# Layer norms that end in their own tile's round, in a four-layer recurrent trunk on one core

## The chip, the core and the metric

The kernel runs on one core of a Trainium2 chip. A core has five engines that run side by side, each with a queue of its own that it works off in order: TensorE (PE in the profile; its weight loads are listed apart as PEld), VectorE (DVE), ScalarE (ACT), GpSimd (POOL) and SyncE (SP), which here only starts transfers. Matrix products are written to PSUM, in eight banks of 128 x 512 numbers; everything else lies in SBUF, 128 partitions wide. Engines wait for one another at semaphores, and a waiting instruction holds up all that is queued behind it on its engine. The metric is device time in microseconds (us) of one execution.

## The reference

One inference step of a trunk over 1024 prompt tokens and 64 sample tokens (8 sequences of 8), with 1024 channels. Two mixers, each followed by a gated convolutional FFN, and after each of the four a layer norm over the channels. Cut to what matters here:

```python
for i in range(DEPTH):                                   # DEPTH = 2
    mix = rglru_mixer(x, ...) if i % 2 == 0 else hgrn2_mixer(x, ...)
    x = layer_norm(ALPHA * x + mix, ln_g[i, 0], ln_b[i, 0])
    f = conv_ffn(x, ...)                                 # 1024 -> 2 x 2816 -> 1024
    x = layer_norm(ALPHA * x + f, ln_g[i, 1], ln_b[i, 1])

def layer_norm(x, g, b):
    mu = mean(x); var = mean((x - mu) ** 2)
    return (x - mu) * rsqrt(var + 1e-5) * g + b
```

The mixers end in a product with a 1024 x 1024 matrix, the FFN in one with 2816 x 1024. All of it is float32 in and out; the kernel splits every operand of a product into a high and a low part and adds three products.

## The kernel before

**Phases.** Phase 0 is the first mixer (up to about 288 us) and its closing norm (to about 350), phase 1 the first FFN (to about 1125), phase 2 the second mixer (to about 1820), phase 3 the second FFN (to the end). Tokens lie in nine tiles: 0 to 7 with 128 prompt tokens each, and tile 8 with the 64 sample tokens. The running sum of a tile is z[:, m], 1024 numbers on each partition, which holds one token.

**A layer norm** is the tail of each of the four parts, and all four go through `ln_pipeline`. A round per tile: `step_m` issues the products of the tile on PE (24 matmuls of 512 columns) and `resid` on DVE, which adds a PSUM bank to z and sums up the row (L433). `nrm_a` (L443 to L446) takes the mean on DVE, squares the row with an accumulated sum on ACT (L444), and forms the reciprocal root by logarithm and exponential (L445, L446). `nrm_b` has four instructions on one number per token (L451 to L454) and (z + mean) * g over the row, in place (L456). `nrm_c` scales the row, adds b, in place (L473), and starts the transfer of the tile to DRAM (L478, or L476 for the output). The order of the tiles is 8, 0, 4, 1, 5, 2, 6, 3, 7 at the two mixers (`sums=True`) and 8, 0, 1, ... 7 at the FFNs.

Before the change the three parts belong to three rounds: in round i stand `nrm_b` of the tile before and `nrm_c` of the one before that, and the turn of the one before that again:

```python
            if 0 <= i - 2 < NT:
                nrm_c(order[i - 2], final)
```

**The turn.** The next part needs channels on partitions. At the first FFN's tail `to_x` transposes a tile on PE (8 transposes, L355), copies the high part on ACT (L357) and the low part on DVE (L358). At a mixer's tail `to_sums` (L363) transposes two tiles mp and mp + 4 (16 transposes, L375), because the FFN's input products are done in a form with seven products of 2 x 2 blocks: it forms seven sums of four blocks b11, b21, b12, b22, in scratch rows t1 to t4 inside z, and writes a high part (ACT, L402) and a low part of each into xa. Four of these sums and three low parts are on DVE, which reads PSUM (L406, L413 to L421), four low parts on POOL (L406).

**PE's order.** PE works in program order, so a turn stands between the products of one tile and those of the next, and waits there for the `nrm_c` of its tile. Turns that are left over are put in `pend` and run in the next part's first product step: the list is emptied by `fill` (one) and `flush` (all). In the FFN's `products` the weights come as seven parts i, and the tokens as two halves c of each token group (columns 0 to 287 and 288 to 543); in the first step c is the outer loop, so (0,0), (1,0), ... (6,0) need the sample tile and the sums of tiles 0, 4, 1, 5 only.

**Weights** come by DMA into `raw` buffers and are converted into a place (`wb`, `wr`, `wxf`, `wxb`): the high part by ACT (L216, L185), the low part by POOL or DVE, by `run["lo"]` (L217, L186). For the FFN's input products each of the seven parts is half a place, and four of them need a sum on POOL first (L176 to L182). `convert` does the next block or part if a place and the raw data are there. Only places of kind "b" are open to a block of the next phase. `pump` is one such try; `release` gives the places of the products done back.

Of the kernel before, what the change touches and what calls it, by code (L numbers as in the profile page):

```python
# [14 lines left out]
ALU = mybir.AluOpType  # L15
# [45 lines left out]
def hawk_hgrn2_convffn_deepnorm_kernel(  # L61
# [301 lines left out]
    def to_sums(mp):  # L363
# [20 lines left out]
        if len(ms) == 2:  # L384


            c0s = ((0, 512, 4096, 4608), (0, 512, 4096, 4608), (8192, 8704, 4096, TW), (2048, 2560, 6144, 6656))[mp]
            s = [zf[:, c0:c0 + 512].rearrange("p (k t) -> p k t", t=n) for c0 in c0s]
        else:
            s = [z[:, ms[0], i * 4 * n:(i + 1) * 4 * n].rearrange("p (k t) -> p k t", t=n) for i in range(4)]  # L390
# [20 lines left out]
        hi(6, b22)  # L411
        lo(0, b11, dve)
# [8 lines left out]
        dve.tensor_tensor(t4, b21, t2, ALU.subtract)  # L421
        hi(5, t4)
        lo(3, t1, pool)
# [24 lines left out]
    def nrm_b(m):  # L448
        r = rows_of(m)
        st = stat[:r, m]  # L450
        dve.tensor_scalar(st[:, 5:6], st[:, 3:4], 1.0 / D, LN_EPS, ALU.mult, ALU.add)  # L451
        dve.scalar_tensor_tensor(st[:, 6:7], st[:, 4:5], st[:, 4:5], st[:, 5:6], ALU.mult, ALU.mult)
        dve.tensor_scalar(st[:, 6:7], st[:, 6:7], -0.5, 1.5, ALU.mult, ALU.add)
        dve.tensor_tensor(st[:, 7:8], st[:, 4:5], st[:, 6:7], ALU.mult)  # L454
        if run.get("end") != m:
            dve.scalar_tensor_tensor(z[:r, m], z[:r, m], st[:, 2:3], gb[:r, 0], ALU.add, ALU.mult)  # L456
            return

        for _, c in END:
            dve.tensor_scalar(z[:r, m, c], z[:r, m, c], st[:, 2:3], st[:, 7:8], ALU.add, ALU.mult)  # L460
        for eng, c in END:
            eng.tensor_tensor(z[:r, m, c], z[:r, m, c], gb[:r, 0, c], ALU.mult)
# [3 lines left out]
    def nrm_c(m, final):  # L466
        r = rows_of(m)
        st = stat[:r, m]
        for eng, c in END if run.get("end") == m else ((dve, slice(0, D)),):
            if run.get("end") == m:  # L470
                eng.tensor_tensor(z[:r, m, c], z[:r, m, c], gb[:r, 1, c], ALU.add)
            else:
                eng.scalar_tensor_tensor(z[:r, m], z[:r, m], st[:, 7:8], gb[:r, 1], ALU.mult, ALU.add)  # L473
# [10 lines left out]
    def ln_pipeline(step_m, junk, final=None, between={}, sums=False):  # L484
# [4 lines left out]
        run["end"] = order[-1] if final == "out" else None  # L489

# [6 lines left out]
        for i in range(NT + 2):  # L497
            def mid():
                if 0 <= i - 1 < NT:
                    nrm_b(order[i - 1])  # L500

            if i < NT:
                if not step_m(order[i], mid):
                    mid()
                pump()
                nrm_a(order[i], junk())
            elif final != "out":

                if i == NT:
                    release(run["held"])  # L510
                lo = run["lo"]
                run["lo"] = pool if sums else dve
                convert()
                mid()
                convert()
                run["lo"] = lo
            if 0 <= i - 2 < NT:
                nrm_c(order[i - 2], final)
            if i >= NT and final == "out":
                mid()  # L520
            run["bank"] = "in"
            if i in between:
                between[i]()
            if final != "out" and 3 <= i < NT:
                turn(order[i - 3])
            run["bank"] = "s"
        if final != "out":
            for m in order[NT - 3:]:
                if not sums or m >= 4:
                    pend.append(lambda m=m: turn(m))  # L530
# [97 lines left out]
    def mix_out(phase, w, z_src, li, es, early=None):  # L628
# [4 lines left out]
        def prod_part(ps, m, ks, ws):  # L633
            if m < NT - 1:
                xt = xm[:, m // 4, :, :, HD + (m % 4) * P:HD + (m % 4 + 1) * P]
                for k in ks:
                    wt = ws[k // 2 - ks[0] // 2]
                    wh = wt[:, 0, (k % 2) * 512:(k % 2 + 1) * 512]
                    wl = wt[:, 1, (k % 2) * 512:(k % 2 + 1) * 512]
                    pe.matmul(ps, lhsT=xt[:, k, 0], rhs=wh, start=(k == 0), stop=False)  # L640
                    pe.matmul(ps, lhsT=xt[:, k, 0], rhs=wl, start=False, stop=False)  # L641
                    pe.matmul(ps, lhsT=xt[:, k, 1], rhs=wh, start=False, stop=(k == KT - 1))  # L642
            else:
                for k in ks:
                    wt = ws[k // 2 - ks[0] // 2]
                    lt = ys[:, k].rearrange("p a b -> p (a b)")
                    for i in range(2):
                        wv = wt[:, i, (k % 2) * 512:(k % 2 + 1) * 512]
                        pe.matmul(ps, lhsT=lt, rhs=wv, start=(k == 0 and i == 0), stop=(k == KT - 1 and i == 1))  # L649
# [64 lines left out]
        def pass1(ws):  # L714
            def step_m(m, mid):
# [5 lines left out]
                if m in (NT - 1, 0):  # L721
                    prod_part(banks[m], m, range(4, KT), ws[2:])
                    resid(m, 1, banks[m], True, acc=True)
                else:
# [286 lines left out]
    def ffn(phase, li, final):  # L1011
# [194 lines left out]
        for p in range(NP):  # L1206
            f0, f1 = 2 * p, 2 * p + 1

            def gates(b, p=p, f0=f0, f1=f1):
# [3 lines left out]
                else:  # L1213
                    fills = {(1, 0): [fill], (5, 0): [flush]}
# [32 lines left out]
        for gi, grp in enumerate(GROUPS):  # L1247
# [27 lines left out]
            else:  # L1275
                def fn(ws, grp=grp):
                    flush()

                    def sm(m, mid):
                        prod(m, 0, grp, [ws[0], ws[2]], False, True)  # L1280
                        mid()
                        prod(m, 1, grp, [ws[1], ws[3]], False, True)
                        return True
# [565 lines left out]
```

## Time and profile before

| what | us |
|---|---|
| median of 3 runs | 2591.05 (2588.37 to 2592.32) |
| the profiled execution | 2598.02 |
| its span, first to last instruction | 2596.2 |
| mean granted TensorE clock in it | 0.982 of full |

In the profile a row of the timeline is: start, duration, engine, line, operation, output <- input, shape, count, and in brackets the idle time of the engine before it with the one that ended it. Neighbouring matmuls overlap in these rows, so a matmul's cost is the distance of two starts. The page names DVE and ACT groups by the line of the helper. Busy times over the whole span: PE 2506.6, DVE 1538.2, POOL 1362.1, ACT 951.2 us.

### The profile page before, as it was taken

The numbers are of one execution on the slowest core, as the hardware profiler recorded it, in microseconds if no ns is written. First come the engines' busy times: TensorE is split into PE (matmuls) and PEld (weight loads), VectorE is DVE, ScalarE is ACT, GpSimd is POOL, SyncE is SP. The second block draws the span as 40 slices with busy tenths as digits, with TensorE's granted clock in tenths as the row PEclk, the third lists the DMA queues.
The fourth block names the chain that finished last, engine by engine and source line by source line (L and its number), as shares of the span: only waits on it lengthen the run. The fifth ranks groups of instructions, "written<-read, shape, count | busy, mean of one in ns | idle before, by whom it ended". The sixth has DMA issues, their size and how long they took to land. (4 is left out here: it accounts for less than half of the span.)

```text
span 2596.2 us, 39881 instructions
## 1 busy us (share of the span) xinstructions
PE 2506.6 (97%) x16007; PEld 2320.0 (89%) x16007; DVE 1538.2 (59%) x2384; ACT 951.2 (37%) x1643; POOL 1362.1 (52%) x1162
## 2 busy tenths in 40 slices
PE   9999979999999999999999999999799999999998
PEld 9999869999999788789999999877699999988886
DVE  5987375565656422568858585976666565662326
ACT  4776243333333111244545353444332333340113
POOL 2534158888876432115444443612788887872321
PEclk9999989999999999999999999999899999999999
DMA  4114122222224422121211111132222222264111
GB/s 132 41 45 161 37 81 63 85 71 84 67 84 166 155 100 83 48 83 45 60 30 49 51 42 51 42 105 83 64 78 83 84 67 84 67 235 153 55 46 73
DMA packets 205839, 209.79 MB, mean 81 GB/s; under 512 B 13201, under 2 KB 167953, under 8 KB 205614
## 3 DMA queue, kind: packets, MB, share of 16 engines
q1 hardware_dynamic: 205654, 207.25, 24.8%
q8 instruction: 126, 2.06, 0.3%
q14 instruction: 59, 0.48, 0.1%
HBM read 159.61 MB, written 47.61 MB: 80 GB/s over the span
## 5 line engine op out<-in xcount | busy, mean ns | idle before, releaser
L217 POOL TENSOR_TENSOR wb<-raw,wb 128x1024 fp32r<-128x1024 f32 (+1 forms) x76 | 199.1, 2622 | 523.1 <-ACT wb L216 293.4
L1084 DVE TENSOR_TENSOR z<-z,ps_f 128x256 f32<-128x256 f32 (+2 forms) x550 | 196.0, 378 | 358.5 <-PE ps_f L1079 301.8
L1079 PE MATMUL ps_f<-xa,wb 128*128 128x288 f32 (+1 forms) x3072 | 402.6, 291 | 4.9 <-POOL xa L406 3.1
L1079 PEld LDWEIGHTS ps_f<-xa,wb 128*128 128x128 f32 x3072 | 394.5, 190 | 8.0 <-POOL xa L406 4.0
L1079 PE MATMUL ps_f<-x,wb 128*128 128x288 f32 (+1 forms) x2496 | 327.4, 291 | 20.7 <-DVE z L1084 18.3
L1079 PEld LDWEIGHTS ps_f<-x,wb 128*128 128x128 f32 x2496 | 322.0, 191 | 21.9 <-DVE z L1084 18.9
L300 PE MATMUL ps_in<-xa,wb 128*128 128x384 f32 (+3 forms) x912 | 307.3, 337 | 8.1 <-ACT y8h L1371 5.9
L302 PE MATMUL ps_in<-xa,wb 128*128 128x384 f32 (+3 forms) x912 | 300.4, 329 | 0.5 <-DVE stat L451 0.5
L301 PE MATMUL ps_in<-xa,wb 128*128 128x384 f32 (+3 forms) x912 | 300.7, 330 | 0.1
L433 DVE SCALAR_TENSOR_TENSOR z<-z,ps_fo 128x512 f32<-128x512 f32 x128 | 87.5, 686 | 288.0 <-PE ps_fo L1184 278.2
L186 POOL TENSOR_TENSOR wb<-raw,wb 128x512 fp32r<-128x512 f32 x116 | 162.4, 1407 | 66.5 <-ACT wb L185 56.2
L186 POOL TENSOR_TENSOR wb<-rawf,wb 128x512 fp32r<-128x512 f32 x116 | 165.6, 1435 | 56.9 <-ACT wb L185 56.9
L300 PEld LDWEIGHTS ps_in<-xa,wb 128*128 128x128 f32 x912 | 173.6, 190 | 12.2 <-ACT y8h L1371 7.3
L1132 DVE SCALAR_TENSOR_TENSOR z<-z,ptf 128x1104 f32<-128x1104 f32 x88 | 182.2, 2070 | 1.6
L301 PEld LDWEIGHTS ps_in<-xa,wb 128*128 128x128 f32 x912 | 173.6, 190 | 1.4 <-DVE xa L358 0.9
L302 PEld LDWEIGHTS ps_in<-xa,wb 128*128 128x128 f32 x912 | 173.3, 190 | 1.6 <-DVE wb L217 1.0
L216 ACT CAST wb<-raw 128x1024 fp32r<-128x1024 f32 (+1 forms) x81 | 79.8, 986 | 233.2 <-issue 119.6
L1079 PE MATMUL ps_f<-xa,wxf 128*128 128x256 f32 (+1 forms) x1152 | 149.8, 288 | 2.6 <-ACT z L1099 2.6
L1079 PEld LDWEIGHTS ps_f<-xa,wxf 128*128 128x128 f32 x1152 | 146.6, 189 | 3.0 <-ACT z L1099 3.0
L185 ACT CAST wb<-rawf 128x512 fp32r<-128x512 f32 x116 | 71.0, 623 | 211.9 <-POOL rawf L182 76.0
L185 ACT CAST wb<-raw 128x512 fp32r<-128x512 f32 x116 | 70.1, 623 | 177.5 <-POOL raw L182 63.7
L1182 PE MATMUL ps_fo<-wb,xa 128*128 128x512 f32 x320 | 126.8, 396 | 3.0 <-DVE z L433 3.0
(508 smaller groups left out, 5664.2 us busy)
## 6 DMA issues: line engine op xcount, KB each, us to landing
raw<-in_ffn_w_in_dram SPq DMA_DIRECT2D x44, 512.0 KB
rawf<-in_ffn_w_in_dram SPq DMA_DIRECT2D x44, 512.0 KB
ysave<-z SPq DMA_DIRECT2D x44, 512.0 KB
raw<-in_hg_w_in_dram SPq DMA_DIRECT2D x32, 512.0 KB
xa<-ysave SPq DMA_DIRECT2D x28, 544.0 KB
zsave<-z SPq DMA_DIRECT2D x24, 512.0 KB
raw<-in_ffn_w_out_dram SPq DMA_DIRECT2D x24, 512.0 KB
z<-zsave SPq DMA_DIRECT2D x24, 512.0 KB
```

What stands on the lines that cost most here:

```text
L185: act.copy(w[:, 0], src)
L186: run["lo"].tensor_tensor(w[:, 1], src, w[:, 0], ALU.subtract)
L216: act.copy(w[:, 0, :n], raw[:, :n])
L217: run["lo"].tensor_tensor(w[:, 1, :n], raw[:, :n], w[:, 0, :n], ALU.subtract)
L300: pe.matmul(ps[:, :n], lhsT=wh, rhs=xh, start=(k == 0), stop=False)
L301: pe.matmul(ps[:, :n], lhsT=wh, rhs=xl, start=False, stop=False)
L302: pe.matmul(ps[:, :n], lhsT=wl, rhs=xh, start=False, stop=(k == KT - 1))
L433: dve.scalar_tensor_tensor(zz, zz, a, ps, ALU.mult, ALU.add, accum_out=stat[:, m, n:n + 1] if acc else None)
L1079: pe.matmul(ps[:, :n], lhsT=l, rhs=r, start=(kk == 0 and i < 4 and l is wh and r is xh), stop=(kk == 3 and l is wl), skip_group_check=(i > ...
L1084: dve.tensor_tensor(d, s, pv(ps), ALU.add)
L1132: dve.scalar_tensor_tensor(c[:, :L], gs[:, i:i + L], w[:, i:i + 1], c[:, :L], ALU.mult, ALU.add)
L1182: pe.matmul(ps, lhsT=yh, rhs=wh, start=a, stop=False)
```

## The change

`ln_pipeline` has no third stage any more. A round issues products, `nrm_a`, `nrm_b`, then the turn of the tile before, then `nrm_c` of its own tile. The four small instructions move from `nrm_b` to `nrm_c`. One turn is left over in `pend` where there were three. In `to_sums` the sum t4 moves from DVE to POOL, for which ACT copies b21 out of PSUM; scratch rows of the first pair move. In the last tile's round at a mixer, the products begin with the weights in places of kind "b", each is given back when its products are issued, and a conversion is tried after two of the four; at an FFN two places are given back between the halves of the last tile.

```diff
-            c0s = ((0, 512, 4096, 4608), (0, 512, 4096, 4608), (8192, 8704, 4096, TW), (2048, 2560, 6144, 6656))[mp]
+            c0s = ((8192, 8704, 0, 512), (0, 512, 4096, 4608), (8192, 8704, 4096, TW), (2048, 2560, 6144, 6656))[mp]
...
         hi(6, b22)
+        act.copy(t4, b21)
...
-        dve.tensor_tensor(t4, b21, t2, ALU.subtract)
+        lo(3, t1, pool)
+        pool.tensor_tensor(t4, t4, t2, ALU.subtract)
         hi(5, t4)
-        lo(3, t1, pool)
...
     def nrm_b(m):
         r = rows_of(m)
+        if run.get("end") != m:
+            dve.scalar_tensor_tensor(z[:r, m], z[:r, m], stat[:r, m, 2:3], gb[:r, 0], ALU.add, ALU.mult)
...
+    def nrm_c(m, final):
+        r = rows_of(m)
         st = stat[:r, m]
         dve.tensor_scalar(st[:, 5:6], st[:, 3:4], 1.0 / D, LN_EPS, ALU.mult, ALU.add)
...
-        for i in range(NT + 2):
...
+        for i, m in enumerate(order):
+            step_m(m)
+            pump()
+            nrm_a(m, junk())
+            nrm_b(m)
+            if i == NT - 1:
+
+                release(run["held"])
                 lo = run["lo"]
                 run["lo"] = pool if sums else dve
-                convert()
-                mid()
-                convert()
+                for _ in range(2):
+                    convert()
                 run["lo"] = lo
...
             if i in between:
                 between[i]()
-            if final != "out" and 3 <= i < NT:
-                turn(order[i - 3])
+            if final != "out" and i:
+                turn(order[i - 1])
             run["bank"] = "s"
+            nrm_c(m, final)
         if final != "out":
-            for m in order[NT - 3:]:
-                if not sums or m >= 4:
-                    pend.append(lambda m=m: turn(m))
+            pend.append(lambda: turn(order[-1]))
...
+                elif m == run["last"]:
+
+                    held = list(run["held"])
+                    js = sorted(range(4), key=lambda j: blocks[held[j]].kind != "b")
+                    ps = sbank("ps_o")
+                    for n, j in enumerate(js):
+                        prod_part(ps, m, (2 * j, 2 * j + 1), [ws[j]], (js[0] * 2, js[3] * 2 + 1))
+                        if blocks[held[j]].kind == "b":
+                            release([held[j]])
+                        if n == 1:
+                            convert()
+                    resid(m, 1, ps, True, acc=True)
...
-                    fills = {(1, 0): [fill], (5, 0): [flush]}
+                    fills = {(3, 0): [flush]}
...
                         prod(m, 0, grp, [ws[0], ws[2]], False, True)
-                        mid()
+                        if m == run["last"]:
+                            release([run["held"][0], run["held"][2]])
+                            convert()
                         prod(m, 1, grp, [ws[1], ws[3]], False, True)
```

More of the change, by code (lines that the diff above doesn't have):

```diff
@@ L449, in nrm_b @@
         r = rows_of(m)
+        if run.get("end") != m:
+            dve.scalar_tensor_tensor(z[:r, m], z[:r, m], stat[:r, m, 2:3], gb[:r, 0], ALU.add, ALU.mult)
+    END = (pool, slice(768, D)), (dve, slice(0, 768))
+    def nrm_c(m, final):
+        r = rows_of(m)
         st = stat[:r, m]
@@ L454, in nrm_b @@
         dve.tensor_tensor(st[:, 7:8], st[:, 4:5], st[:, 6:7], ALU.mult)
[L455 to L462, printed above, removed]
-    END = (pool, slice(768, D)), (dve, slice(0, 768))
-    def nrm_c(m, final):
-        r = rows_of(m)
-        st = stat[:r, m]
+        if run.get("end") == m:
+            for _, c in END:
+                dve.tensor_scalar(z[:r, m, c], z[:r, m, c], st[:, 2:3], st[:, 7:8], ALU.add, ALU.mult)
+            for eng, c in END:
+                eng.tensor_tensor(z[:r, m, c], z[:r, m, c], gb[:r, 0, c], ALU.mult)
         for eng, c in END if run.get("end") == m else ((dve, slice(0, D)),):
@@ L489, in ln_pipeline @@
         run["end"] = order[-1] if final == "out" else None
+        run["last"] = order[-1]
         def turn(m):
@@ L495, in turn @@
                 to_sums(m - 4)
-        for i in range(NT + 2):
[L498 to L503, printed above, removed]
-                    mid()
[L505 to L510, printed above, removed]
+        for i, m in enumerate(order):
[5 more added lines that the diff above has]
+                release(run["held"])
                 lo = run["lo"]
                 run["lo"] = pool if sums else dve
-                convert()
-                mid()
-                convert()
+                for _ in range(2):
+                    convert()
                 run["lo"] = lo
[L517 to L520, printed above, removed]
             run["bank"] = "in"
@@ L631, in mix_out, with prod_part @@
         banks = {}
-        def prod_part(ps, m, ks, ws):
+        def prod_part(ps, m, ks, ws, ends=(0, KT - 1)):
             if m < NT - 1:
@@ L639, in prod_part @@
                     wl = wt[:, 1, (k % 2) * 512:(k % 2 + 1) * 512]
-                    pe.matmul(ps, lhsT=xt[:, k, 0], rhs=wh, start=(k == 0), stop=False)
+                    pe.matmul(ps, lhsT=xt[:, k, 0], rhs=wh, start=(k == ends[0]), stop=False)
                     pe.matmul(ps, lhsT=xt[:, k, 0], rhs=wl, start=False, stop=False)
-                    pe.matmul(ps, lhsT=xt[:, k, 1], rhs=wh, start=False, stop=(k == KT - 1))
+                    pe.matmul(ps, lhsT=xt[:, k, 1], rhs=wh, start=False, stop=(k == ends[1]))
             else:
@@ L648, in prod_part @@
                         wv = wt[:, i, (k % 2) * 512:(k % 2 + 1) * 512]
-                        pe.matmul(ps, lhsT=lt, rhs=wv, start=(k == 0 and i == 0), stop=(k == KT - 1 and i == 1))
+                        pe.matmul(ps, lhsT=lt, rhs=wv, start=(k == ends[0] and i == 0), stop=(k == ends[1] and i == 1))
         def prod(m, n, ws):
@@ L714, in pass1, with step_m @@
         def pass1(ws):
-            def step_m(m, mid):
+            def step_m(m):
                 if m == NT - 1:
@@ L1277, in fn, with sm @@
                     flush()
-                    def sm(m, mid):
+                    def sm(m):
                         prod(m, 0, grp, [ws[0], ws[2]], False, True)
-                        mid()
+                        if m == run["last"]:
+                            release([run["held"][0], run["held"][2]])
+                            convert()
                         prod(m, 1, grp, [ws[1], ws[3]], False, True)
-                        return True
                     ln_pipeline(sm, lambda: fs_["junk"], final, {1 + 2 * g: (lambda g=g: states(g)) for g in range(3)})
```

## The prediction, made before the changed kernel was run

> **What bounds the kernel now.** I read the busy shares first, then PE's waits by the line waited for (total, times, longest), then PE's timeline where those waits lie.
>
> ```profile
> PE 2506.6 (97%) x16007; PEld 2320.0 (89%) x16007; DVE 1538.2 (59%) x2384; ACT 951.2 (37%) x1643; POOL 1362.1 (52%) x1162
> ...
> PE ps_f L1079 <- DVE z L1084: 18.3, 2, 10.1
> PE ps_t L375 <- DVE z L473: 14.2, 4, 5.0
> ```
>
> PE is busy almost throughout, so what counts is what adds to its 90 us of idle time or takes from it. The two largest waits are at one place that occurs twice: where a mixer's closing norm passes into the FFN. PE there, first occurrence: the last tile's products start at 339.71, the first seven FFN products run from 345.38 to 384.04; the last row is a stretch of 4 us:
>
> ```profile
> 338.86 1.09 PE L375 MATMUL ps_t<-ident,z 128*128 128x128 f32 x8 [2.13 <-DVE z L473]
> ...
> 339.71 0.48 PE L640 MATMUL ps_o<-wr,xa 128*128 128x512 f32 x1
> ...
> 345.38 1.94 PE L1079 MATMUL ps_f<-xa,wb 128*128 128x288 f32 x13
> ...
> 376.51 3.25 PE L1079 MATMUL ps_f<-x,wb 128*128 128x288 f32 x12 [8.18 <-DVE z L1084]
> ...
> 384.04 1.69 PE L1079 MATMUL ps_f<-xa,wb 128*128 128x256 f32 x13
> 386.56 4.45 PE L1079 MATMUL ps_f<-xa,wb 128*128 128x256 f32 x35 [0.82 <-POOL xa L406]
> ...
> 356.00:360.00 4.00, 3.95 (x17) 3.60 (x17) 3.55 (x5) 0.82 (x3) 3.07 (x2) 0.50 0.32 131
> ```
>
> From the last norm product to the end of (6,0), 345.38 to 384.04, pass 38.7 us. At full clock the work is 7 x 1.69 + two turns of 1.7 = 15.2 us; the rest, 23.5, is idle time (8.18 in the row of 376.51, and L375's longest wait of 5.0) and, after that, a clock of 0.50 (the stretch row's column behind POOL). The waits come twice each, so some 47 us are on offer at the two places. The question is whether DVE, which ends those waits, is relieved. Its rows in a round there, with ACT and POOL between:
>
> ```profile
> 325.69 1.28 DVE L473 SCALAR_TENSOR_TENSOR z<-z,stat,gb 128x1024 f32<-128x1024 f32 x1
> ...
> 334.97 1.31 POOL L406 TENSOR_TENSOR x<-z,x 128x512 fp32r<-128x512 f32 x1
> ...
> 335.25 1.04 DVE L454 TENSOR_TENSOR stat<-stat 128x1 f32<-128x1 f32 x1
> 336.21 1.27 DVE L456 SCALAR_TENSOR_TENSOR z<-z,stat,gb 128x1024 f32<-128x1024 f32 x1
> 337.41 0.20 DVE L443 TENSOR_SCALAR stat<-stat 128x1 f32<-128x1 f32 x1
> ...
> 337.65 1.15 ACT L444 ACTIVATE junk<-z,stat 128x1024 f32<-128x1024 f32 x1 [4.23 <-DVE stat L443]
> 338.70 0.19 ACT L444 ACTIVATION_READ_ACCUMULATOR junk<-z,stat 128x1 f32 x1
> 338.73 0.68 DVE L433 SCALAR_TENSOR_TENSOR z<-z,ps_o 128x512 f32<-128x512 f32 x1
> 339.25 0.20 ACT L446 ACTIVATE stat<-stat 128x1 f32<-128x1 f32 x1
> ...
> 340.02 0.16 DVE L454 TENSOR_TENSOR stat<-stat 128x1 f32<-128x1 f32 x1
> ...
> 341.42 1.28 DVE L473 SCALAR_TENSOR_TENSOR z<-z,stat,gb 128x1024 f32<-128x1024 f32 x1
> ```
>
> DVE is already the bound of these rounds: from one L473 to the one two rounds on, 325.69 to 341.42, pass 15.7 us, where PE needs 2 x 5.6 + 1.7 = 12.9. And it goes from L443 over an L473 of 1.2 to the next L433 (338.73) while ACT still squares, because `nrm_b` and `nrm_c` belong to earlier tiles.
>
> **The change part by part.**
>
> *The added wait.* L456 writes z in place, and L444 reads z. With both in one round, L456 cannot start before the square is over: 337.41 to 338.89 in the rows, 1.5 us after L443 starts. DVE has nothing else to do in that time, as its queue is in order; behind L456 stand the turn's low parts, the small ones, L473, and the next tile's resid, and PE's transposes wait for L473. The trace has no L456 that waits so. Bounds: nothing, if the wait ended with L443; 2.0 us, if it reached to L446's end. I take 1.5, the end of the reads.
>
> One tile's chain is then resid 0.7 + 1.5 + L456 1.2 + four small 0.65 + L473 1.2 = 5.3 us (distances of starts), plus the turn's part of DVE before the small ones.
>
> *First FFN's tail (turn of every tile).* The rows of before:
>
> ```profile
> 1071.68 0.20 DVE L443 TENSOR_SCALAR stat<-stat 64x1 f32<-64x1 f32 x1
> 1071.98 2.40 POOL L217 TENSOR_TENSOR wb<-raw,wb 128x1024 fp32r<-128x1024 f32 x1 [2.80 <-ACT wb L216]
> ...
> 1104.57 0.82 ACT L1198 COPY so<-ps_fs 18x512 f32<-18x512 f32 x2
> ...
> 1108.04 1.03 PE L355 MATMUL ps_t<-ident,z 128*128 128x128 f32 x8
> 1112.90 1.29 DVE L358 TENSOR_TENSOR xa<-ps_t,xa 128x512 fp32r<-128x512 f32 x2 [1.16 <-ACT xa L357]
> ...
> 1121.61 0.47 PE L300 MATMUL ps_in<-xa,wb 128*128 128x512 f32 x1
> ...
> 1128.33 1.23 DVE L217 TENSOR_TENSOR wb<-raw,wb 128x1024 fp32r<-128x1024 f32 x1
> ...
> 1139.58 0.36 PE L300 MATMUL ps_in<-xa,wb 128*128 128x256 f32 x1
> ```
>
> PE needs 6.4 us a round (1108.04 to 1121.61 is two rounds and a turn of 0.8) and does not wait. With the change DVE's round is two resids 1.4 + 1.5 + 1.2 + L358 1.2 + 0.65 + 1.2 = 7.2 to 7.3, and 8.05 in the rounds where L1198's copies stand ahead of the turn's high parts on ACT. PE may now be only one round ahead of a tile's L473, so DVE's pace becomes PE's. From the rows: tile 8 has L443 at 1071.7; its L456 comes behind POOL's L217 (until 1074.4), its L473 ends at 1077.4. Then tile 0 (state copies, short turn) 7.6, tile 1 7.3, tile 2 8.05, tile 3 7.3, tile 4 8.05, tiles 5 and 6 7.3 each: tile 6 ends at 1130.3, its transposes at 1131.1, and only then the next part's first product, which began at 1121.61. 1.6 us of that are two turns that only come earlier. Tile 7's L473 stands behind both conversions (two L217 of 1.2) and ACT's two casts, at 1140.4 by the same steps; PE's first product ends at 1136.6, so its transposes wait 3.8. Two products (5.55 and 2.85) and the turn follow: the row of 1139.58 comes at 1149.5. **+9.9 us.** Bounds: if the wait cost nothing, DVE's round is 5.7, below PE's 6.4, and only the wait before the last turn is left, +2; with L446's end and every round slowed, +13. The early release of two places here gives nothing: they are wxf and wxb (kind "x"), and the next phase's block takes kind "b".
>
> *The output's tail (no turn).*
>
> ```profile
> 2539.76 0.20 DVE L443 TENSOR_SCALAR stat<-stat 64x1 f32<-64x1 f32 x1
> ...
> 2585.57 0.21 DVE L443 TENSOR_SCALAR stat<-stat 128x1 f32<-128x1 f32 x1
> ...
> 2588.09 0.15 DVE L451 TENSOR_SCALAR stat<-stat 128x1 f32<-128x1 f32 x1
> ```
>
> PE's round is 5.6 (6.4 without the turn). DVE's becomes 1.4 + 1.5 + 1.2 + 0.65 + 1.2 = 6.0 to 6.1. Tile 8's L473 ends 4.65 after 2539.76, at 2544.4; then 1.45 and seven rounds of 6.1: the last L443 at 2588.55, 3.0 late. The last L451 came 2.5 after its L443, where L446 ends after 2.0; two L473 stood between, and that goes. **+2.5 us** (bounds +0.5 and +4). PE is not held: it may be four PSUM banks ahead.
>
> *The two mixers' tails.* What goes: one of DVE's seven PSUM operations in a turn (0.7), the waits of L456 and L473 for each other's rounds, and one turn out of the first FFN step. What comes: 1.5 a tile, and L473 now lies behind the turn, while POOL runs five operations of 1.3 almost in a row (t4 among them, and hi(5) on ACT waits for it). In the rows L454 took 1.04 while such a POOL operation ran, ending with it, and 0.16 without: so L452, L454 and L473 each wait for one, about 2.5 us in all. A round with a turn: 5.3 + six operations of 0.68 as L433's, with an estimated 0.8 of waiting for ACT's copies, 4.9 + 2.5 = 12.7; without: 5.35. A pair takes 18 us, not 15.7. Step by step at the first place:
>
> ```profile
> 298.52 0.21 DVE L443 TENSOR_SCALAR stat<-stat 64x1 f32<-64x1 f32 x1
> ...
> 299.64 0.40 PE L640 MATMUL ps_o<-wr,xa 128*128 128x512 f32 x1
> ...
> 301.16 1.29 POOL L186 TENSOR_TENSOR wb<-raw,wb 128x512 fp32r<-128x512 f32 x1 [2.94 <-ACT wb L185]
> ```
>
> Tile 8's L473 ends at 304.2 (298.5 + 1.5 + 1.2 + 0.65 + 1.2 and 1.2 for POOL's operation at 301.16), where PE goes from tile 0 to tile 4 at 299.64, so the short turn, now in that round, costs PE a new wait of 4.3 or so; tiles 0, 4: 311.5, 316.9; tile 1 329.6, 5 335.0, 2 347.7, 6 353.1, 3 365.8. The last tile's products start at 354.0 behind the turn of tiles 2 and 6 (before: 339.71, with that turn still to come) and end at 359.6, 14 us later than now. Then the weights:
>
> ```profile
> 356.25 0.60 ACT L185 CAST wb<-raw 128x512 fp32r<-128x512 f32 x1
> 356.93 1.27 POOL L186 TENSOR_TENSOR wb<-raw,wb 128x512 fp32r<-128x512 f32 x1 [3.63 <-ACT wb L185]
> ```
>
> The place for part 2 is free early, at about 357, but L178 stands on POOL behind the turn's last operation (367.0). 1.3 + 0.7 + 1.2: part 2 is ready at 370.2, against 358.2. Part 3 follows at 373.4, tile 7's norm (its square is behind two casts on ACT) ends at 378.5, then the last transposes and (4,0), (5,0), (6,0) at 1.7 each: 384.5. Against 384.04, with the wait of 0.82 at 386.56 gone: **about 0 a place**. So the tail becomes shorter by just what the rounds become longer. Bounds: without POOL's hindrance (2.5 in three turns) -7.5, with a slower clock after the new waits +4.
>
> *Sum:* 0 + 0 + 9.9 + 2.5 = +12.4 us on the profiled 2598.0 (span 2596.2 and 1.8 around it), 2610.4. That execution lies 7 above the median of the runs, 2591.05; on their scale **2603 us**.
>
> **A rule that speaks against the change** is the one of the clock. The rows:
>
> ```profile
> 188.26 0.69 PE L836 MATMUL ps_ri<-xcs,wb 128*128 128x384 f32 x1 [3.64 <-DVE xcs L824]
> 188.75 0.52 PE L837 MATMUL ps_ri<-xcs,wb 128*128 128x384 f32 x1
> ...
> 195.11 0.34 PE L301 MATMUL ps_in<-xa,wb 128*128 128x384 f32 x1
> ```
>
> After 3.64 us of idle time equal matmuls take 0.52, and 0.34 seven us later; after the 2.13 above they were not slower (1.09 for 8 transposes, 1.03 in the row of 1108.04). The Trainium skill, page "TensorE: Matmul & The Clock Gate", section "HAM oscillation — how this bites in real kernels", wants no idle gap over about 3.4 us, as the clock then falls to half until a further window is busy. The trace agrees in both rows. By that rule the new waits of 4.3 and about 4.5 each cost PE some 2 us more, and my sum, which takes them as hidden behind DVE, would be up to 8 us higher at the two places together.
>
> **The rivals.**
>
> *A. The turns run dry of waits (faster).* If DVE's pair of rounds came down to PE's 12.9 us (the square's wait filled, POOL not in the way), PE would reach the last tile some 2 us sooner than now, and the transition would keep only the weights: (6,0) at about 363, -21 a place, -30 in all: 2561. It decides from a pair of 15.0 us on, below today's 15.7: there both places give 9 back, in all -5.6: 2585. For it: 47 us lie there, and today DVE idles for ACT in a turn (1.16 in the row of 1112.90), which the new order fills. Against it: 2 x 1.5 added, and POOL's row of operations moved in front of L473. 0.11.
>
> *B. No change.* The pair stays at 15.7; both places give 7 back each, against +12.4: 2590. This is also what results if the last tile's early places do what they are for and part 2 is ready before the turn's end. 0.17.
>
> *C. Slower than forecast.* The clock falls in the new waits and the slow products delay DVE's next resid in turn: +4 a place and +13 at the FFN's tail: 2615 and above. 0.14.
>
> *My forecast*, +5 to +20: 0.58.
>
> **How the numbers follow.** The range 2587 to 2614 takes in the forecast's bounds and most of B. A measurement here can tell 0.2% (5.2 us) from no change: faster 0.11 (A), same 0.17 (B), slower 0.72 (forecast and C).
>
> **What would show it.** Right: L456 starting 1.5 us after L443 in every round, idle before it ended by ACT L444; at the first FFN's tail PE waits of about 1 us for L473 at the transposes, eight rounds long; the last L451 some 2.5 us further from the last product. At the mixers: a wait of 4 at the short turn, two of about 4 at the long ones, one of 8 to 9 before (2,0), none of 8 before (5,0). Wrong: a pair of rounds under 15 us, or no waits at the first FFN's transposes.

## The result, and the profile after

The changed kernel takes 2616.24 us (median of 4 runs, 2615.91 to 2619.42) against 2591.06 (2588.37 to 2592.32): ratio 1.0101, 95% interval 1.0084 to 1.0119. It is slower by 25 us, where +12 was forecast, and lies above the forecast's range of 2587 to 2614. The profiled execution took 2616.09 us, with a span of 2614.3.

The profiles of before and after differ by 18 us of span, the medians by 25. A second profile of the kernel before settles most of that: its span is 2592.5, and the comparisons below use it. The page of after, and its table of PE's waits (total, times, longest):

```profile
PE 2511.2 (96%) x16007; PEld 2322.0 (89%) x16007; DVE 1546.3 (59%) x2374; ACT 955.7 (37%) x1653; POOL 1373.5 (53%) x1172
```

```profile
PE ps_t L375 <- DVE z L473: 17.9, 6, 4.4
PE ps_t L355 <- DVE z L473: 9.7, 7, 3.2
PE ps_t L382 <- DVE z L473: 8.0, 2, 4.4
PE ps_f L1080 <- ACT wb L185: 6.0, 2, 3.1
...
PE ps_f L1080 <- ACT z L409: 1.7, 2, 0.9
PE ps_f L1080 <- POOL xa L406: 1.7, 2, 0.8
...
PE ps_f L1080 <- DVE z L416: 1.4, 2, 0.7
```

(L1080 is L1079 of before.) The two waits of 8 to 10 us for `DVE z L1084` are gone, as forecast. In their place stand waits for L473 at three lines of transposes, and, in the last three rows, short waits at the FFN's products of the second half of the tokens, which the forecast did not have.

PE issues the same 16007 matmuls in both kernels, so its stages can be compared by the start of the n-th one. Between the 1651st and the 2241st lies the first mixer's closing norm, between the 6301st and the 7051st the first FFN's tail, between the 10731st and the 11541st the second mixer's norm, from the 15601st to the end of the span the output's tail:

| stage, us | before, second profile | after | difference | forecast |
|---|---|---|---|---|
| first mixer's norm | 121.30 | 126.68 | +5.4 | 0 |
| first FFN's tail | 148.30 | 158.05 | +9.75 | +9.9 |
| second mixer's norm | 167.75 | 171.98 | +4.2 | 0 |
| output's tail | 105.19 | 108.17 | +3.0 | +2.5 |
| all else | 2049.9 | 2049.4 | -0.5 | 0 |
| span | 2592.5 | 2614.3 | +21.9 | +12.4 |

So the two tails came out as worked out, and the whole miss is at the mixers.

### The profile page after: what moved, and what is told of

The parts are those of the page before. It is cut to its first block, busy times and chain, and to the rows that moved or that the text cites. A ratio compares the mean times of both kernels' runs of the same rounds, so it can differ in the third digit from the quotient of the medians.

```text
span 2614.3 us, 39899 instructions
## 1 busy us (share of the span) xinstructions
PE 2511.2 (96%) x16007; PEld 2322.0 (89%) x16007; DVE 1546.3 (59%) x2374; ACT 955.7 (37%) x1653; POOL 1373.5 (53%) x1172
## 5 line engine op out<-in xcount | busy, mean ns | idle before, releaser
L1080 PE MATMUL ps_f<-xa,wb 128*128 128x288 f32 (+1 forms) x3072 | 405.8, 292 | 12.3 <-ACT wb L185 6.0
L1080 PEld LDWEIGHTS ps_f<-xa,wb 128*128 128x128 f32 x3072 | 398.2, 192 | 15.5 <-ACT wb L185 6.5
L1080 PE MATMUL ps_f<-x,wb 128*128 128x288 f32 (+1 forms) x2496 | 322.6, 289 | 3.0 <-ACT z L1092 3.0
L1080 PEld LDWEIGHTS ps_f<-x,wb 128*128 128x128 f32 x2496 | 318.0, 189 | 3.4 <-ACT z L1092 3.4
L1080 PE MATMUL ps_f<-xa,wxf 128*128 128x256 f32 (+1 forms) x1152 | 149.8, 288 | 2.7 <-ACT z L1100 2.7
L1080 PEld LDWEIGHTS ps_f<-xa,wxf 128*128 128x128 f32 x1152 | 146.6, 189 | 3.1 <-ACT z L1100 3.1
```

The source lines that it names most:

```text
L1080: pe.matmul(ps[:, :n], lhsT=l, rhs=r, start=(kk == 0 and i < 4 and l is wh and r is xh), stop=(kk == 3 and l is wl), skip_group_check=(i > ...
```

## The experiments

Each kernel differs from the changed one by what its diff shows, the two-stage kernels (two and those named after it) by what is added to the one before. "Early places" are the places that the last tile's round gives back ahead of time. In the names sq stands for ACT's copies of a turn ahead of the square, dve for t4 on DVE, ne for no early places at the mixers, late for the save of tile 7 behind the next loads, sum for a sum of the weights put earlier on POOL. Where the FFN's rounds aren't the new ones, its early places are left out too. In the table stand the stages of each profiled execution against the second profile of before. The same stage in kernels that have the same code there repeats within about 2 us; only the first FFN's tail with the new rounds scatters more, from 9.6 to 12.6, for a reason shown below.

| kernel | time, us | ratio (95%) | mixer 1 | FFN tail | mixer 2 | output |
|---|---|---|---|---|---|---|
| changed | 2616.24 | 1.0101 (1.0084 to 1.0119) | +5.4 | +9.75 | +4.2 | +3.0 |
| ffn_old | 2604.63 | 1.0049 (1.0030 to 1.0068) | +6.0 | +0.1 | +4.3 | 0.0 |
| mix_old | 2606.66 | 1.0053 (1.0036 to 1.0070) | -0.8 | +9.6 | -0.1 | +2.9 |
| sq_gb | 2608.18, one run | | +2.9 | +11.5 | +0.9 | -0.7 |
| ffn_turn_first | 2608.48, one run | | +5.4 | +3.4 | +4.0 | +2.9 |
| clock | 2619.40, one run | | +4.4 | +11.2 | +4.7 | +3.0 |
| new_t4_dve | 2608.92, one run | | +2.5 | +12.4 | +1.0 | +2.9 |
| new_noearly | 2608.32, one run | | +0.7 | +11.3 | -0.7 | +3.0 |
| new_ne_t4 | 2611.01, one run | | +1.1 | +11.6 | -0.8 | +2.9 |
| late_save | 2608.41, one run | | +2.4 | +12.6 | +2.1 | +3.0 |
| repaired | 2604.03 | 1.0045 (1.0031 to 1.0059) | +0.7 | +4.8 | +1.3 | +2.9 |
| two | 2585.43 | 0.9974 (0.9965 to 0.9984) | -2.9 | +0.4 | -2.6 | -0.7 |
| two_sq | 2587.26 | 0.9980 (0.9971 to 0.9990) | -2.3 | +0.4 | -2.8 | -0.7 |
| two_dve | 2581.71 | 0.9964 (0.9951 to 0.9978) | -5.4 | +0.4 | -5.8 | -0.7 |
| two_sq_dve | 2579.58 | 0.9953 (0.9940 to 0.9965) | -7.4 | +0.7 | -8.0 | -0.7 |
| two_sq_dve_late | 2569.64 | 0.9914 (0.9901 to 0.9928) | -12.0 | +0.7 | -11.6 | -0.7 |
| two_sq_dve_ne | 2569.60 | 0.9916 (0.9903 to 0.9930) | -11.8 | +2.3 | -12.5 | -0.7 |
| two_sq_dve_ne_sum | 2566.03 | 0.9904 (0.9889 to 0.9919) | -12.5 | +0.7 | -12.7 | -0.7 |

### Which tails hold the loss

> The kernel before once more, for a second profile. The profiled execution of before lay 7 us above the median of its runs. If that was chance, this profile lies at 2588 to 2592, and the missing 7 us lie outside the four tails (in the first 200 us, where after is 1.1 us quicker, and at the end of the first FFN's input products, where it gains 2.4). If the tails of before themselves scatter, this profile is shorter in one of them.

> The changed kernel with the rounds of before at the two FFN tails alone. Theory (DVE's round with the wait for the square sets PE's pace, place by place): the 9.6 and 3.0 us of these tails go, the mixers' 5.3 and 3.7 stay: 2600 to 2604, PE's waits for L473 at L355 gone. Rival (the loss is carried from the mixers, as the slow clock or late weights, and only shows at the FFN): nothing or little comes back, 2611 to 2616.

> The changed kernel with the rounds, the sum t4 and the last tile of before at the two mixers, the new rounds at the FFNs. Theory: the FFN tails' 9.6 and 3.0 us are all that is left: 2602 to 2606. Rival (the mixers hold most of the loss, since medians differ by 25 us and the profiles by 18): 2595 to 2599.

The second profile is 3.7 us shorter than the first, and 2.7 of that lie in one place, not one of those expected: at the first output products of the FFN (the last section has its rows). For the other two kernels the loop has both forms, and a tail takes the one named (first ffn_old, then mix_old, which also has t4 and the last tile of before):

```diff
+    STYLE = dict(sums='new', ffn='old', out='old')
...
+    STYLE = dict(sums='old', ffn='new', out='new')
```

Both medians, 2604.63 and 2606.66, lie 0.6 and 0.7 us above the theory's ranges and outside the rivals'. Each place loses its own us, and restoring it returns them there and nowhere else: the rival of a loss that is carried on falls. (mix_old holds the FFN's and the output's 12.5, ffn_old the mixers' 10.3.)

### The FFN's tail: two gates of one length

A round of after on DVE and ACT, from one L473 to the next, 7.27 us:

```profile
1086.16 1.28 DVE L473 SCALAR_TENSOR_TENSOR z<-z,stat,gb 128x1024 f32<-128x1024 f32 x1
...
1088.69 0.21 DVE L444 TENSOR_SCALAR stat<-stat 128x1 f32<-128x1 f32 x1
1088.94 1.15 ACT L445 ACTIVATE junkf<-z,stat 128x1024 f32<-128x1024 f32 x1 [4.10 <-DVE stat L444]
1090.22 1.28 DVE L452 SCALAR_TENSOR_TENSOR z<-z,stat,gb 128x1024 f32<-128x1024 f32 x1 [1.31 <-ACT junkf L445]
1090.65 1.05 ACT L357 CAST xa<-ps_t 128x512 fp32r<-128x512 f32 x2
1091.42 1.28 DVE L358 TENSOR_TENSOR xa<-ps_t,xa 128x512 fp32r<-128x512 f32 x2
...
1093.43 1.28 DVE L473 SCALAR_TENSOR_TENSOR z<-z,stat,gb 128x1024 f32<-128x1024 f32 x1
...
1142.35 1.09 PE L355 MATMUL ps_t<-ident,z 128*128 128x128 f32 x8 [3.18 <-DVE z L473]
```

L452 starts 1.53 us after L444, as forecast, and the last transposes wait 3.2 where 3.8 was forecast. sq_gb takes that wait away:

> The changed kernel, but ACT's square reads the row of g in place of z (so the variance, and with it the output, is not that of the reference). It takes as long, but the first pass over z need not wait for it. Theory (the 1.5 us a tile is what makes DVE slower than PE): DVE's round at the FFN tail falls below PE's 6.4, the first FFN's tail loses about 2 us instead of 9.7, the output's tail 0 instead of 3.0; at the mixers a pair of rounds falls from 18 to about 15 and each place is 8 to 10 us shorter: 2584 to 2592 in all. Rival (POOL's operations in front of the last pass, and the turn in the same round, cost the mixers theirs): the two tails as above, the pair stays at 17 to 18: 2600 to 2606.

```diff
-        act.activation(junk[:r, :D], z[:r, m], AF.Square, bias=st[:, 2:3], scale=1.0, accum_out=st[:, 3:4])
+        act.activation(junk[:r, :D], gb[:r, 0], AF.Square, bias=st[:, 2:3], scale=1.0, accum_out=st[:, 3:4])
```

Its round, in the same view (L478 is L473 of after):

```profile
1084.18 1.28 DVE L478 SCALAR_TENSOR_TENSOR z<-z,stat,gb 128x1024 f32<-128x1024 f32 x1
...
1086.71 0.21 DVE L444 TENSOR_SCALAR stat<-stat 128x1 f32<-128x1 f32 x1
1086.96 1.28 DVE L452 SCALAR_TENSOR_TENSOR z<-z,stat,gb 128x1024 f32<-128x1024 f32 x1
...
1088.67 1.05 ACT L357 CAST xa<-ps_t 128x512 fp32r<-128x512 f32 x2
1089.28 1.29 DVE L358 TENSOR_TENSOR xa<-ps_t,xa 128x512 fp32r<-128x512 f32 x2 [1.03 <-ACT xa L357]
...
1091.30 1.28 DVE L478 SCALAR_TENSOR_TENSOR z<-z,stat,gb 128x1024 f32<-128x1024 f32 x1
```

L452 follows at once, but L358 now waits 1.03 for the high parts, which stand on ACT behind square, logarithm and exponential: 2.57 us from L444 to L358, against 2.73 in after, and a round of 7.12 against 7.27. The theory that the wait alone set the round fell: the tail still loses 11.5, and 2608.18 lies above both ranges. At the output, which has no turn and so no second gate, the loss went from +3.0 to -0.7 as expected. At the mixers, too, only 2.5 and 3.3 us came back, not 8 to 10.

> The changed kernel, where at the first FFN's tail the turn of the tile before stands between the mean of a tile (L444) and its square. Reading z was no gate by itself: without it the low parts wait for ACT's copies, which stand behind square, logarithm and exponential. Here the copies come first and the low parts fill DVE's wait for the square. Theory (two gates of the same length, ACT's order and the square): the round is 1.4 + 0.2 + about 2.0 + 1.2 + 0.65 + 1.2 = 6.6 us, PE's pace of 6.4, and the tail loses 2 to 3 us instead of 9.7: 2607 to 2610. Rival (DVE must wait for the square whatever comes first, and the low parts add 1.2 to it): rounds of 7.3 to 8, no gain: 2614 to 2618.

```diff
         dve.tensor_scalar(st[:, 2:3], st[:, 0:1], st[:, 1:2], -1.0 / D, ALU.add, ALU.mult)
+        if mid:
+            mid()
         act.activation(junk[:r, :D], z[:r, m], AF.Square, bias=st[:, 2:3], scale=1.0, accum_out=st[:, 3:4])
```

A round on DVE:

```profile
1100.17 0.21 DVE L444 TENSOR_SCALAR stat<-stat 128x1 f32<-128x1 f32 x1
1100.50 1.29 DVE L358 TENSOR_TENSOR xa<-ps_t,xa 128x512 fp32r<-128x512 f32 x2
1102.12 1.29 DVE L454 SCALAR_TENSOR_TENSOR z<-z,stat,gb 128x1024 f32<-128x1024 f32 x1 [0.34 <-ACT junkf L447]
```

(`mid` is the turn of the tile before, given at the first FFN's tail alone; L454 is L452 of after.) The low parts lie in the wait for the square, of which 0.34 us is left, and the tail loses 3.4. Both gates had to go at once, by order alone.

Why this tail scatters is seen behind the wait for its last transposes, 3.18 us in after (the last row of its round above) and 3.20 in late_save, which has the same code there. A stretch of 4 us behind it, in after and then in late_save:

```profile
1145.00:1149.00 4.00, 4.00 (x20) 3.30 (x19) 0.00 (x0) 0.01 (x1) 0.00 (x0) 1.00 0.44 127
```

```profile
1140.00:1144.00 4.00, 4.00 (x11) 3.08 (x11) 1.10 (x2) 0.54 (x1) 0.00 (x0) 0.55 0.59 154
```

In after and mix_old the granted clock is 1.00 through the whole tail, and they lose 9.75 and 9.6. With 3.4 us at 0.50 there (clock, new_noearly, new_ne_t4) the loss is 11.2 to 11.6, with 6.8 us (new_t4_dve, late_save) 12.4 and 12.6. sq_gb has 6.8 us of it too, so its +11.5 belongs beside the last two: the wait that it takes away gave about 1 us, which is seven rounds of 0.15.

### The mixers: neither the clock nor the rounds

> The changed kernel with 30 and twice 28 transposes of the unit matrix (about 3.8 and 3.6 us) in PE's queue ahead of the three transposes at each mixer that wait 4.4, 4.4 and 3.5 us, into the bank that these write next. Theory (DVE's chain and then the weights set the end of the first half; the slow clock costs 1.2 us at tile 4 and stands in front of a wait else): clock 1.0 after the three waits, the last product some 2 us earlier, the wait before the third FFN product longer by as much, the whole 1 to 3 us a place shorter: 2610 to 2615. Rival C of the prediction (the half clock is what costs the mixers their 4 to 5 us): 2605 to 2608.

At the long turns, and likewise with 30 at the short one:

```diff
+                    for j in range(28 if mp in (1, 2) and m == ms[1] and hb == 0 else 0):
+                        pe.transpose(pv[:, j % 4], ident, ident)
```

Two stretches behind the waits, in after and then in this kernel (the column behind POOL's is the granted clock), and PE's wait for part 2 of the weights in each:

```profile
303.00:307.00 4.00, 3.37 (x14) 2.77 (x15) 2.63 (x5) 2.35 (x9) 0.00 (x0) 0.50 0.30 66
...
356.00:360.00 4.00, 4.00 (x11) 3.11 (x11) 3.18 (x4) 3.60 (x9) 0.00 (x0) 0.57 0.04 11
```

```profile
303.00:307.00 4.00, 2.88 (x20) 2.24 (x19) 2.59 (x6) 1.58 (x4) 0.00 (x0) 1.00 0.30 66
...
356.00:360.00 4.00, 4.00 (x18) 3.20 (x18) 3.25 (x5) 3.37 (x8) 0.18 (x1) 1.00 0.00 0
```

```profile
369.49 0.72 PE L1080 MATMUL ps_f<-xa,wb 128*128 128x288 f32 x2 [3.11 <-ACT wb L185]
```

```profile
369.16 0.85 PE L1132 MATMUL ps_f<-xa,wb 128*128 128x288 f32 x2 [5.58 <-ACT wb L185]
```

After an idle time of 4.4 us the trace of after has a clock of 0.50. That is the rule of the Trainium skill, page "TensorE: Matmul & The Clock Gate", section "HAM oscillation — how this bites in real kernels", and the trace agrees. But with full clock restored the products end earlier only to wait longer, 5.58 for 3.11, and the two mixers lose 9.1 us together where they lost 9.6. The whole, 2619.40, lies above the ranges of theory and rival. Rival C falls at the mixers.

> The changed kernel with the sum t4 on DVE again, as before the change. Theory (t4 on POOL takes 0.7 us from DVE's turn but puts a fifth POOL operation beside DVE's passes over z, so it gives about nothing): pair of rounds 17.5 to 18.7, whole within 2 us of the changed kernel. Rival (t4 on POOL is what lengthens the rounds): pair 16.5 or less, 4 to 8 us shorter.

> The changed kernel without the early places in the last tile's round (products in the order of the weights, nothing given back ahead of time). Theory (part 2 waits on POOL behind the turn, not for a place): the time within 2 us of the changed kernel. Rival (the early place is what keeps the loss at the mixers to 4 or 5 us): 3 to 6 us a place more, 2622 to 2628.

The edits: t4 is again `dve.tensor_tensor(t4, b21, t2, ALU.subtract)` and ACT's copy is left out; and, for the other kernel,

```diff
-                elif m == run["last"]:
+                elif False:
...
-                        if m == run["last"]:
+                        if False:
                             release([run["held"][0], run["held"][2]])
```

Of t4 the size is the rival's, 7 us, but not its mechanism: the pair of rounds stays at 18.3 (the waiting transposes start at 334.98 and 353.28). The other run went against theory and rival: without the early places the mixers' loss is gone, +0.7 and -0.7: **the early places cost 5 us at each mixer**. How, is seen in the timeline of ACT, DVE, SP and PE at the first mixer's end. After:

```profile
372.05 0.62 ACT L185 CAST wb<-raw 128x512 fp32r<-128x512 f32 x1 [2.61 <-POOL raw L180]
372.58 1.15 ACT L445 ACTIVATE junk<-z,stat 128x1024 f32<-128x1024 f32 x1
...
377.56 1.28 DVE L473 SCALAR_TENSOR_TENSOR z<-z,stat,gb 128x1024 f32<-128x1024 f32 x1
...
379.29 1.45 SPq L140 DMA_DIRECT2D rawf<-in_ffn_w_in_dram  x2
...
383.99 0.62 ACT L185 CAST wxf<-rawf 128x512 fp32r<-128x512 f32 x1 [3.20 <-DMA rawf<-in_ffn_w_in_dram]
384.52 0.58 ACT L402 CAST xa<-ps_t 128x512 fp32r<-128x512 f32 x1
...
385.64 1.80 PE L1080 MATMUL ps_f<-xa,wb 128*128 128x256 f32 x12 [0.84 <-ACT z L409]
388.15 0.35 PE L1080 MATMUL ps_f<-xa,wb 128*128 128x256 f32 x1 [0.71 <-DVE z L416]
389.34 0.86 PE L1080 MATMUL ps_f<-xa,wb 128*128 128x256 f32 x5 [0.84 <-POOL xa L406]
```

Without early places, the same view (L478 and L1127 are L473 and L1080 of after):

```profile
367.03 1.15 ACT L445 ACTIVATE junk<-z,stat 128x1024 f32<-128x1024 f32 x1 [1.32 <-DVE stat L444]
...
369.39 0.85 PE L1127 MATMUL ps_f<-xa,wb 128*128 128x288 f32 x2 [3.31 <-ACT wb L185]
...
372.01 1.28 DVE L478 SCALAR_TENSOR_TENSOR z<-z,stat,gb 128x1024 f32<-128x1024 f32 x1
...
373.74 1.45 SPq L140 DMA_DIRECT2D rawf<-in_ffn_w_in_dram  x2
...
379.04 0.62 ACT L185 CAST wxf<-rawf 128x512 fp32r<-128x512 f32 x1
379.57 0.58 ACT L402 CAST xa<-ps_t 128x512 fp32r<-128x512 f32 x1
```

An early place lets two conversions be issued before tile 7's norm. Their casts wait on ACT for sums on POOL, in front of tile 7's square, which is at 372.58 and not at 367.03. Tile 7's last pass follows 5.55 later. SP saves that row before it loads the next weights (`rawf`), so the load is issued 5.55 later; ACT's cast of them waits 3.20 us for it, and the last turn's copies stand behind that cast: 384.52 and not 379.57. It is there that PE loses most of its time, at the products of the last turn's sums; before that it waits 1.3 us at the last transposes (378.90) for tile 7's late norm. Part 2 of the weights, which the early place is for, comes no earlier: PE goes on at 369.49 here and at 369.39 without.

> The changed kernel, with the transfer that saves tile 7 at a mixer's end issued on SP after the FFN's third product, behind the loads of the next weights, in place of at the end of tile 7's norm. Theory (SP's queue: the load of rawf stands behind that save, which waits for tile 7's L473; ACT's cast of rawf waits 3.2 us for the load, and the last turn's copies stand behind the cast): the load is issued some 5 us earlier, the cast follows POOL's sum at once, the last turn's first copy comes some 3 us earlier, and each place is 3 us shorter: 2608 to 2612. Rival (the last turn is late because tile 7's norm is late, whatever SP does): 2614 to 2618.

```diff
+                if run["sums"] and m == 7:
+                    run["late"] = save
+                else:
+                    save()
...
-                    fills = {(3, 0): [flush]}
+                    fills = {(3, 0): [flush, lambda: run["late"]()]}
```

In the timeline of SP and ACT there:

```profile
365.60 1.45 SPq L140 DMA_DIRECT2D rawf<-in_ffn_w_in_dram  x2
...
379.40 0.62 ACT L185 CAST wxf<-rawf 128x512 fp32r<-128x512 f32 x1
379.92 0.58 ACT L402 CAST xa<-ps_t 128x512 fp32r<-128x512 f32 x1
```

The load goes out 13.7 us earlier, the cast no longer waits, and the mixers lose 2.4 and 2.1 where they lost 5.4 and 4.2. So SP's queue holds 3.0 us of the first mixer's loss, as the theory had it, and 2.1 of the second's. Against the kernel without early places 1.7 and 2.8 are left; there PE waits 1.1 and 2.3 us for tile 7's last pass at the last transposes, which it does not do without early places, so the late square is likely the rest.

> The changed kernel without the early places and with t4 on DVE again. t4 on DVE gave 2.5 to 3.2 us a place beside the early places. Theory (POOL's queue ends with the turn's last operation, ahead of part 2's sum, so t4's 1.3 us and its way over ACT count with or without early places): 2 to 3 us a place less than the run without early places, 2601 to 2605. Rival (t4 cost only because the early places had used up the slack): as without early places, 2606 to 2610.

The mixers go with the rival: +1.1 and -0.8, as with t4 on POOL. The time, one run, lies 1 us above the rival's range. t4 cost 2.9 and 3.2 only beside the early places; that it did so in the same chain is not shown.

> The changed kernel without the early places of the last tile, and with the turn ahead of the square at the first FFN's tail. Theory (parts add up: mixers as before, -0.2 and -0.7 as in the run without early places; first FFN's tail +2 to +4; output's tail +3): 2596 to 2600. Rival (the parts hang together): outside of that.

The parts add up but for the FFN's tail, +4.8 where 2 to 4 was expected, and the second mixer's +1.3: 2604, above the range. At the FFN's tail this execution has 3.4 us at a clock of 0.50 (from 1076.0), which ffn_turn_first, with +3.4, does not have. Repaired so, the change is still 0.45% slower than before; ending a norm in its own round has gained nothing at any of the four places.

### A version that beats both

> The changed kernel with two stages in place of one or three: all of a tile's norm on DVE in the round after its own, the turn in the round after that; t4 on POOL, the mixers' last tile as changed. No instruction waits for the square. Theory (the wait of 1.5 us a tile is what costs): the FFN's round is PE's 6.4 again, the mixers' pair falls to about 15.0 or below, and 9 us a place come back against before: 2570 to 2586. Rival (POOL in front of the norm and the order of the weights' conversion cost the mixers their gain, not the wait): mixers as in the changed kernel, FFNs as before: 2598 to 2604.

```diff
+            def mid():
+                if 0 <= i - 1 < NT:
+                    nrm_s(order[i - 1])
+                    nrm_b(order[i - 1])
...
+            if 0 <= i - kc < NT:
+                nrm_c(order[i - kc], final, False)
...
+            if final != "out" and kc + 1 <= i < NT:
+                turn(order[i - kc - 1])
```

(`nrm_s` holds the four small instructions, and `kc` is 1.)

2585.43, the upper edge of the range: 2.7 us a place rather than 9, since the pair of rounds came to 16.5 us (its last passes at 331.27 and 347.81) and not to 15.0.

> The two-stage kernel with ACT's copies of a mixer's turn ahead of the square of the tile just done, and in the last round the turn ahead of one conversion, with DVE in POOL's place for the low parts of the weights. In the two-stage kernel DVE waits 1.15 us in each turn for copies that stand behind a square, and 4.0 us in the last one behind two casts. If these waits are on the path: 3 to 5 us a place less than with two stages, 2576 to 2581. If POOL or the weights end last there: same as two stages, 2583 to 2588.

```diff
         hi(6, b22)
         act.copy(t4, b21)
+        if hook:
+            hook()
...
+                if first and i == NT - 1:
+                    run["lo"] = dve
```

(`hook` is `nrm_a` of the tile just done.) No gain over two stages: at the first mixer the copies of the turn of tiles 2 and 6 come earlier, and PE then waits 4.4 us for the weights' fourth part.

> The two-stage kernel with the sum t4 on DVE. Theory from the run with t4 on DVE in the changed kernel (2.5 to 3.2 us a place, since POOL's queue stands between the turn and the weights): the same gain here, 2578 to 2582. Rival (with two stages ACT's queue ends last, not POOL's): as the two-stage kernel, 2583 to 2588.

> The two-stage kernel with the turn's copies ahead of the square, the turn ahead of a conversion in the last round, and t4 on DVE. In the run with t4 on POOL the FFN's fourth product waited 4.4 us for weights that stood behind the turn on POOL. Theory: that wait falls to 2 or less and each place gains 2 to 3 us: 2580 to 2583. Rival (the end of the place is set by the last turn's sums, three waits of 0.8): 2584 to 2588.

With t4 on DVE the one gains 2.5 and 3.2 us a place, as the theory had it, the other 5, where 2 to 3 was expected.

> The best version so far (two stages, the turn's copies ahead of the square, t4 on DVE) without the early places of the last tile. Theory (the early places put casts ahead of tile 7's square on ACT and so delay its norm, its save on SP, and the load and the turn behind them): the FFN's last transposes wait less than the 3.5 us of now, 2 to 4 us a place less, 2572 to 2576. Rival (here the turn already stands ahead of the second conversion, and the early places bring the weights forward): 2580 to 2585.

> The best version so far with the save of tile 7 behind the loads of the next weights on SP. If ACT waits for such a load there too: 1 to 3 us a place less, 2574 to 2578. If not: the same, 2578 to 2581.

Taking the early places away, or taking the save out of SP's way, gives 10 us in all, more than either expectation, which fits a chain that either breaks. In two_sq_dve_ne a pair of rounds is 14.05 us (329.69 to 343.74).

> The best version so far, with POOL's sum for part 2 of the FFN's first weights (L178) right behind part 1, in front of the turns, where POOL is idle for 9 us. Before the third FFN product PE waits 6.3 us for that part, whose sum stands behind the last four POOL operations of the turn. Theory: the cast follows the turn's copies at about 353.5, the wait falls from 6.3 to 1 to 2 us, and what ends next are part 3 and tile 7's norm: 2 to 4 us a place less, 2562 to 2566. Rival (part 3 takes its place at once): 2567 to 2570.

Part 2 came early, and PE's wait for it fell from 6.3 to 0.9; the next wait, 3.9 us for part 3, took its place: the rival's mechanism. The time, 2566.03 (2562.10 to 2568.53), cannot be told from two_sq_dve_ne's (2567.02 to 2571.46). Both kernels are about 0.9% faster than before. PE's first waits in two_sq_dve_ne:

```profile
PE ps_f L1136 <- ACT wb L185: 11.4, 2, 6.3
...
PE ps_f L1136 <- DVE z L417: 4.9, 2, 2.5
...
PE ps_t L375 <- DVE z L479: 2.7, 4, 0.9
```

What is left there is the weights' way through POOL and ACT; DVE's norms hold PE up by no more than 0.9 us at a time.

## Why the prediction was right in sign and short in size

- **The added wait** was right: 1.53 us after L444 in the row, 1.5 forecast. But "if the wait cost nothing, DVE's round is 5.7" was wrong: without it the round was 7.12 (sq_gb), because ACT's order is a second gate. The lower bound of +2 rested on that; only the other order came near it, with +3.4.
- **First FFN's tail**, +9.9: +9.75, in rounds of 7.27 where 7.2 to 7.3 was forecast. The pace was right; that the tail fits within 0.2 us is in part luck, as the sum has no price for a half clock behind the last wait, and where an execution has it the loss is 11.2 to 12.6. **Output's tail**, +2.5: +3.0; there the wait alone is the cause.
- **The mixers' rounds**, "about 0 a place": right as far as the rounds go, +0.7 and -0.7 without the early places. A pair of rounds took 18.0 us, as forecast, and the step-by-step times held as well (forecast, then measured): short turn's wait 4.3 and 4.4, tile 7's norm at 378.5 and 378.8, (6,0)'s end at 384.5 and 384.8. One sign missed: the wait before (2,0) was 3.1 and not 8 to 9. The last tile's products, begun at a clock of 0.50, ran from 355.6 to 363.0, 7.4 us where 5.6 was forecast, and at full clock, in the kernel clock, the wait was 5.6. As the weights end last there, this changed nothing behind it.
- **The step that failed** is the end of the sum there: "Against 384.04, with the wait of 0.82 at 386.56 gone: about 0 a place". It stopped at (6,0). The working had tile 7's square behind two casts and its norm late, but not what else waits for that norm: the save on SP, the load behind it, the cast that waits for the load, and the last turn behind the cast. Three waits (0.84, 0.71, 0.84) came where one of 0.82 was to go, and a stretch of half clock behind them: 5.4 and 4.2 us. The stretch is the smaller part: the kernel clock does not have it and still loses 4.4 and 4.7. At the mixers the early places were given no price of their own; without them +0.7 and -0.7 is left, so their price is the whole of it, within the scatter.
- **Rival C** had the right size, and its mechanism is not the cause at the mixers. At the FFN's tail it is not in the profile of after either (clock 1.00); in other executions it adds 1.5 to 3 us there. Rival B's second way, that the early places do their work, is out: they are what costs.
- **The rest.** +12.4 forecast and +9.6 at the mixers make 22, the difference of the profiles. The medians show 25; the kernel before had medians of 2590.3 to 2592.8 beside the later runs, and its second profiled execution took 2594.23, so some 3 us of that are its scatter.

## What to carry to other kernels

When a buffer is given back early, follow every instruction that this lets into a queue, and on each engine ask what is now behind it: here two casts stood in front of a square, the square in front of a save, the save in front of a load. When a wait is to be removed, look for the next gate of the same length before pricing the gain, and remove it with the order of the same few instructions. A stage between producer and consumer (as in the kernel two) can cost nothing, where having none costs a wait in each round. And before a few microseconds of one execution are put down to a change, its granted clock in that stage is worth a look.

## What was not expected of the hardware

DVE's pass over a tile takes longer beside POOL. In after, the timeline of DVE and POOL at the first mixer:

```profile
328.02 1.29 POOL L423 TENSOR_TENSOR z<-z 128x512 f32<-128x512 f32 x1
...
328.11 2.28 DVE L473 SCALAR_TENSOR_TENSOR z<-z,stat,gb 128x1024 f32<-128x1024 f32 x1
```

2.28 us for 1.28 in the FFN's rows above: nearly all of the overlap is lost. By the Trainium skill, page "SBUF — State Buffer", section "SBUF: two separate sides", the two engines share a port pair, and of a DVE instruction with two inputs in SBUF and a POOL one that reads SBUF, whichever starts first has it for its whole instruction. The rows agree: POOL started first, and DVE's pass ends 1.0 us late.

The clock can fall after less than 2 us of idle time. The first profile of before, PE's timeline at 861.87, and the stretch of 4 us behind it:

```profile
861.87 0.50 PE L1182 MATMUL ps_fo<-wb,xa 128*128 128x512 f32 x1 [1.99 <-DVE z L433]
```

```profile
864.00:868.00 4.00, 4.00 (x14) 3.14 (x13) 4.00 (x6) 0.00 (x0) 4.00 (x3) 0.68 1.02 409
```

The second profile, the same two:

```profile
860.24 0.50 PE L1182 MATMUL ps_fo<-wb,xa 128*128 128x512 f32 x1 [0.85 <-DVE z L433]
```

```profile
864.00:868.00 4.00, 4.00 (x19) 3.13 (x18) 4.00 (x5) 0.00 (x0) 3.64 (x3) 1.00 1.03 409
```

The same kernel, and 2.7 us apart at this one place: 1.1 of waiting, the rest a clock of 0.68. The Trainium skill, page "TensorE: Matmul & The Clock Gate", section "HAM oscillation — how this bites in real kernels", wants no idle gap over about 3.4 us; here 1.99 was enough, and the measurement decides. Nor does a wait of one length always have the same effect: behind 3.18 us at the first FFN's last transposes after kept 1.00, behind 3.20 late_save fell to 0.55. What decides is not shown here. Part of the scatter between executions comes about so.
